# Retention values of all four heads projected in one unit of 512-column products, and gate units in another order, in a hybrid retention and block-attention layer

## Chip, cores and metric

The kernel runs on one core of a Trainium2 chip, as one program. The metric is the device time of one execution in microseconds (us).

## What is computed

The reference is one decoder layer for 512 tokens of width 1024, in float32. Cut to what matters:

```python
h = rmsnorm(x, norm1_w)
rq, rk, rv, rg, mq, mk, mv, ga, gb = split(h @ w_in)      # 512 512 1024 1024 512 512 512 1024 1024 columns
ret = silu(rg) * retention(rotary(rq), rotary(rk), rv)    # 4 heads, key width 128, value width 256
a = ret @ w_ret_out
b = moba_attention(rmsnorm(mq), rmsnorm(mk), mv) @ w_moba_out   # 8 heads of width 64
x = x + (sigmoid(ga) * a + sigmoid(gb) * b) @ w_o
h2 = rmsnorm(x, norm2_w)
x = x + (silu(h2 @ w_ffn_gate) * (h2 @ w_ffn_up)) @ w_ffn_down
```

The retention values `rv` are 1024 columns of `h @ w_in`, 256 for each head. The retention of a head takes scores of its rotated queries and keys (`rq`, `rk`), weights them by decay, and multiplies them with its values. The gates `ga` and `gb` are needed where `a` and `b` are mixed.

## The kernel before

**The units.** Everything outside attention and retention is a matrix product, and the kernel cuts it into units. Most units are one 2-by-2 block product done in seven block products instead of eight (Winograd's form of Strassen's method), named B11, B21, T1, T2, B22, T3 and T4. A block product takes its weights as one "piece" (or two) of 128 x 1024 numbers, which a DMA brings from HBM into a raw tile (`raw`); for T1 and T3 a second DMA on GpSimd's queue adds another quarter to it. To keep float32 accuracy, each piece is split into a rounded high part (`wh`, a cast on ScalarE, L418) and the rest (`wl`, a subtraction on VectorE, L222); the activations are held in the same two parts, and each product is three matmuls (`mm3`, L467): high by high, high by low, low by high. All matmuls, and all VectorE operations, are recorded at L222, a helper's line.

**Shapes.** For most units a matmul streams 256 columns. A unit of kind W (`rk`, `ga`, `gb`) holds the weights still and streams 256 tokens. A unit of kind X (`rv`, `rg`) holds tokens still and streams 256 columns of weights. A unit of 256 columns does 7 block products of 24 matmuls, 168 in all. A "wide" X unit (`mv` with the first half of `rg`, L1479, and the output projections) streams 512 columns and covers twice the columns with the same 168 matmuls; each of its block results takes two banks of PSUM instead of one, and its pieces are twice as many.

**The order of the work.** The code is written out in the order in which each engine runs it (the schedule is manual, and every engine takes its instructions in the order of the code). `ORDER` (L45) lists the units between attention's inputs and the output projection. Inside a unit, a string such as `NORMAL` (L80) gives the order of the seven products; what stands behind the slash (T4) is run inside the next unit, at its `*1`. Behind every half block product, that is 12 matmuls of 256 columns, comes one slot: `advance` (L435) takes a step of the clock called tick here, prepares at most one more piece, and `run_bg` (L718) takes one item from the list `bg`. The work of attention and of retention stands in that list, so that it is spread over the units; `later(n, f)` (L263) puts f off by n ticks. In the feed units `b` and `a` (`feat_blocks`, L753) a slot comes behind 12 matmuls of 512 columns.

**Attention** starts behind the `mv` unit, as 38 steps (`att_step`, L1159): products with masks, VectorE's row maximum (`mx`, `nb`), ScalarE's exponential (`p`, L1108), VectorE's scaling, TensorE's transposes into PSUM (`ps`), ScalarE's copies of them (`pt`, L1140 and L1145), and products with the values. PSUM has eight banks here, handed round; a unit that starts needs a bank that attention has given back.

**Retention before.** The unit `rv` 0 gives the values of heads 0 and 1, `rv` 1 those of heads 2 and 3. When the last quarter of such a unit is out (`rv_out`, L1258), the scores (`ret_scores`, L1285) and products (`ret_values`, L1315) of its two heads go into `bg`. By then the rotated queries and keys of those heads (`rk` 0 or `rk` 1, `rot_out`, L1216, tiles `rot`, `rH`, `rL`) have long been ready, for `rk` stands ahead of `rv`. When all is in, `ret_finish` (L1374) adds the normalisation (`ret_norm`) and the transposes (`ret_transpose`) into the tiles `ret`, which `a` multiplies.

**Gates.** `gate_unit` (L1395) multiplies each quarter by the token's norm on VectorE (`qa`, `qb` by `r1b`) and takes a tanh on ScalarE (L1405).

Of the kernel before, what the change touches and what calls it, by code (L numbers as in the profile page):

```python
# [13 lines left out]
ALU = mybir.AluOpType  # L14
# [25 lines left out]
STARTERS = 2  # L40
EXTRA = 1
WIDE = 4
OEXTRA = 5
FEXTRA = -2
ORDER = (("rk", 0), ("rv", 0), ("gb", 0), ("rk", 1), ("rv", 1), ("rg", 1), ("gb", 1), ("b", 0), ("b", 1), ("ga", 0), ("a", 0), ("ga", 1), ("a", 1))  # L45
RLAG = (1, 2, 3)
SLAG = (1, 1, 1)
ROT = 1
# [32 lines left out]
ENDING = "B11 T1 *1 T2 B21 B22 T3 T4w"  # L81
PLAIN = "B11 B21 B12 B22"
DOWN = "B11 B21 T1 T2 B22 T3 / T4"
ALONE = "B11 B21 T1 T2 B22 T3 T4z"


def weight_plan():

    units = []

    def feat(blocks):
        assert len(blocks) % 16 == 0  # L100
        for i in range(0, len(blocks), 16):
            units.append(("F", blocks[i:i + 16]))

    def group(name, col, kts):
        return [(name, k * P, col) for k in range(kts)]

    def wino(name1, col1, name2, col2, order=NORMAL):
        quarters = ((name1, col1, 0), (name2, col2, 0), (name2, col2, 4), (name1, col1, 4))
        units.append(("W", [(n, (k0 + k) * P, c + i * P) for n, c, k0 in quarters for i in (0, 1) for k in range(4)],
                      order))  # L110

    halves = (range(4), range(4, 8))

    def cols(col):
        units.append(("X", ("w_in", halves, (col, col + 256), 256), NORMAL))

    units += [("M", (C_MQ, 0)), ("M", (C_MQ, 4)), ("M", (C_MK, 0)), ("M", (C_MK, 4))]
    units.append(("X", ("w_in", halves, (C_MV, C_RG), 512), NORMAL))
    for name, i in ORDER:
        if name == "rg":  # L120
            cols(C_RG + 512 * i)
        elif name == "rv":
            cols(C_RV + 512 * i)
        elif name == "rk":
            wino("w_in", C_RQ + 256 * i, "w_in", C_RK + 256 * i)
        elif name == "a":
            feat(sum([group("w_ret_out", (4 * i + ct) * P, KT) for ct in range(4)], []))
        elif name == "b":
            feat(sum([group("w_moba_out", (4 * i + ct) * P, 4) for ct in range(4)], []))
        else:  # L130
            c = {"ga": C_GA, "gb": C_GB}[name] + 512 * i
            wino("w_in", c + 256, "w_in", c)
    units.append(("X", ("w_o", halves, (0, 512), 512), ALONE))
    for c in range(len(CHUNKS)):
        fs = chunk_tiles(c)
        for f in fs[::2]:
            order = ENDING if f == fs[-2] else NORMAL
            if f < 4:
                order = (PLAIN, DOWN)[f // 2]
            wino("w_ffn_gate", f * P, "w_ffn_up", f * P, order)  # L140
        units.append(("X", ("w_ffn_down", (fs[::2], fs[1::2]), (0, 512), 512), ALONE if c == len(CHUNKS) - 1 else DOWN))
    return units
# [27 lines left out]
def hybrid_block(ctx: ExitStack, tc: tile.TileContext, wall, xin, xtok, n2, cin, out):  # L170
# [652 lines left out]
    def wino_unit(w, ev, hooks={}):  # L823

        u = cur[0]
        cur[0] += 1
        order = plan[u][2].split()
        wide = plan[u][0] == "X" and plan[u][1][3] == 512
        banks = {}

        def bank(b):
            if b not in banks:
                z = zbank if b == "Z" else main_ps()
                banks[b] = [z, zbanks.pop() if b == "Z" and len(zbanks) > 1 else main_ps()] if wide else z
            return banks[b]

        def third(*x):
            ev.c22(*x)
            if "T4w" in order:
                ev.u3(*x)  # L840

        def first(*x):
            ev.p1(*([*x, bank("Z")] if seed else x))

        whole = "T4w" in order or "T4z" in order
        seed = order[1] != "B21"
        table = {"B11": ("X", "A11", True, False, first), "T1": ("Y", "S1", True, False, ev.p5),
                 "T2": ("X", "S2", False, False, ev.u2), "B21": ("Z", "A12", not seed, True, ev.c11),
                 "B22": ("Y", "S4", False, True, ev.c12), "T3": ("X", "S3", False, whole, third),
                 "T4": ("X", "A22", False, True, ev.c21),  # L850
                 "T4w": ("W", "A22", True, True, getattr(ev, "c21w", None)),
                 "T4z": ("Z", "A22", False, True, ev.c21)}

        def run(q):
            b, m, start, stop, out = table[q]
            wino_prod(w, u, bank(b), m, q.rstrip("wz"), start, stop, out,
                      (lambda i: ev.u3(bank("X"), i, bank("Z"))) if q == "T3" and "T4z" in order else None,
                      q == "T4z")

        rest = False  # L860
        for q in order:
            if q == "/":
                rest = True
            elif q[0] == "*":
                for _ in range(int(q[1:])):
                    wino_finish()
            elif rest:
                wpend.append(lambda q=q: run(q))
            else:
                run(q)  # L870
                if q in hooks:
                    hooks[q]()
# [53 lines left out]
    class WideQuarters:  # L926


        def __init__(self, out):
            self.out = out  # L930
            self.tiles = big(nm("qa")), big(nm("qb"))
            self.a, self.b = ((t[:, :512], t[:, 512:]) for t in self.tiles)

        def p1(self, x, i, z):
            A.copy(z[i], x[i])

        def p5(self, y, i):
            A.activation(self.a[i], y[i], AF.Copy, scale=-1.0)
# [2 lines left out]
            A.activation(self.b[i], x[i], AF.Copy, scale=-1.0)  # L941

        def c11(self, z, i):
            self.out(0, 0, i, z[i])

        def c12(self, y, i):
            V.tensor_tensor(self.b[i], self.b[i], y[i], ALU.subtract)
# [268 lines left out]
    def rot_out(h0):  # L1216
        def f(r, c, x):

            a, b = halves(nm("rot"))
            hf = RDK // 2  # L1220
            cos, sin = (y[:, r * 256:(r + 1) * 256].unsqueeze(1).to_broadcast([P, 2, 256]) for y in (cosT, sinT))
            part = {}

            def turn():
                A.copy(b[:hf], x[hf:])
                A.copy(b[hf:], x[:hf])

            def same():
                V.tensor_tensor(two(a), two(x), cos, ALU.mult)

            def high():
                if (c, h0) not in rT:
                    H, L = big(f"rH{c}_{h0}", F32R), big(f"rL{c}_{h0}", F32R)
                    rT[c, h0] = H, L
                    for i in (0, 1):
                        s = slice(i * 512, (i + 1) * 512)
                        (rqT, rkT)[c][h0 + i] = Two(H[:, s], L[:, s])
                part["H"], part["L"] = (two(y)[:, :, r * 256:(r + 1) * 256] for y in rT[c, h0])
                A.copy(part["H"], two(a))

            d = lane_start(LANE)
            if c == 0 or d == 0:
                turn()
            else:
                later(d, turn)
            later(1 if c == 0 else d + 1, same)
            later(d + 1, lambda: V.tensor_tensor(two(b), two(b), sin, ALU.mult))
            later(d + 2, lambda: V.tensor_tensor(a, a, b, ALU.add))
            later(d + 3, high)
            later(d + 4, lambda: V.tensor_tensor(part["L"], two(a), part["H"].bitcast(F32), ALU.subtract))  # L1250
        return f

    rqT, rkT = {}, {}
# [1 line left out]

    rv = {}

    def rv_out(h0):  # L1258
        def f(pair, i, x):
            rv[h0 + i, pair] = split(f"rv{h0 + i}_{pair}", x, None, 0 if i == 0 else SLAG[1])  # L1260
            if (pair, i) == (1, 0):
                a, b = ([lambda h=h, j=j: ret_scores(h, j) for j in range(NT)] for h in (h0, h0 + 1))
                v, w = ([lambda h=h, p=p: ret_values(h, p) for p in range(2)] for h in (h0, h0 + 1))
                fs = gates(h0 // 2)
                bg.extend(a + fs[:3] + v + b + [fs[3], None, None] + w + [None])
                ret_done("rv")
        return f


    sk = small("sk", RH * NT, 1)  # L1270
# [44 lines left out]
    def ret_values(h, pair):  # L1315
        ps = side_ps()
        for i in (2 * pair, 2 * pair + 1):
            c = (i % 2) * 256
            for j in range(i + 1):
                key, off = sc_off[j]  # L1320
                o = off + (i - j) * P
                mm3(ps[:, c:c + 256], tuple(x[:, o:o + P] for x in sc[h, key]),
                    rv[h, j // 2][:, (j % 2) * 256:(j % 2) * 256 + 256], j == 0, j == i)
        def stats():
            for i in (0, 1):
                bs = tp.tile([P, 6], F32, name=nm("bs"), tag="bs", bufs=4)
# [55 lines left out]

    def rk_unit(n):
        wino_unit(hW, Quarters(rot_out(2 * n)))

    def rv_unit(n):
        wino_unit(hW, Quarters(rv_out(2 * n)))


    sga, sgb, mixT = {}, {}, {}  # L1390
# [74 lines left out]
    def branch(cts, n, mov, evac):  # L1465
# [2 lines left out]
        feat_blocks(blocks[:n] + [wino_finish] + blocks[n:])  # L1468

    make = {  # L1470
        "rg": rg_unit, "rk": rk_unit, "rv": rv_unit,
        "ga": lambda n: gate_unit(sga, 4 * n),
        "gb": lambda n: gate_unit(sgb, 4 * n),
        "a": lambda n: branch(range(4 * n, 4 * n + 4), KT, retT, a_evac),
# [4 lines left out]
    wino_unit(hW, mv_ev)  # L1479
    more_raws(-WIDE)  # L1480
    for name, n in ORDER:
        make[name](n)
    assert not bg


# [362 lines left out]
```

## Time and profile before

| | |
|---|---|
| median of 3 runs | 778.76 us (778.73 to 779.47) |
| the profiled execution, its own time | 778.7 us |
| its span in the trace | 776.9 us, so 1.8 us lie around it |
| TensorE busy (PE) | 770.0 us of the span, 5224 matmuls |
| VectorE busy (DVE) | 630.8 us |
| ScalarE busy (ACT) | 454.9 us |
| granted TensorE clock | 1.00 |
| DMA | 134.85 MB, 174 GB/s on average |

PE is TensorE multiplying, PEld its loading of the stationary operand, DVE VectorE, ACT ScalarE, POOL GpSimd, SP the engine that issues most DMAs. A row of the timeline gives the start in us, the duration in us, the engine, the line, the operation, what it writes and reads, its form, and how many were merged; in brackets stands idle time ahead of it and who ended it. The durations of matmuls overlap, so the cost of one in a stream is read from start to start.

### The profile page before, as it was taken

What the parts mean: (1) busy time and instruction counts of PE and PEld (TensorE: products, weight loads), DVE (VectorE), ACT (ScalarE), POOL (GpSimd) and SP (SyncE); (2) the same over time, 40 slices, a digit from 0 to 9 for tenths busy, and PEclk for the clock granted to TensorE, in tenths of its full rate; (3) what the DMA queues carried; (4) which work ended last, traced back from release to release, by engine and by line L of the source; (5) the groups of instructions that cost most, each with busy time, mean ns of one, the idle gap of its engine ahead of it and who ended that gap; (6) DMA issues with size and microseconds to landing.
All of it is one profiled execution on the core that took longest, in us unless ns stands there. A gap on an engine that the chain in (4) does not pass through costs nothing.

```text
span 776.9 us, 13317 instructions
## 1 busy us (share of the span) xinstructions
PE 770.0 (99%) x5224; PEld 702.0 (90%) x5224; DVE 630.8 (81%) x959; ACT 454.9 (59%) x746; POOL 68.9 (9%) x83
## 2 busy tenths in 40 slices
PE   9999999999999999999999999999999999999997
PEld 6888888889999998989988899989999899988995
DVE  7988688887797677758589898899787977789786
ACT  8656587876675485734356675645554455655451
POOL 0001000000101000000001000111001110110000
PEclk9999999999999999999999999999999999999999
DMA  9947542536768474654899614779556993779502
GB/s 329 359 120 188 129 83 62 140 104 159 192 167 199 118 216 114 166 133 130 249 330 258 171 41 110 193 200 297 157 146 153 271 261 99 174 202 293 119 2 109
DMA packets 40959, 134.85 MB, mean 174 GB/s; under 512 B 4544, under 2 KB 5568, under 8 KB 40896
## 3 DMA queue, kind: packets, MB, share of 16 engines
q1 hardware_dynamic: 29088, 94.41, 34.3%
q0 software_dynamic: 11376, 39.06, 28.7%
q8 instruction: 41, 0.67, 0.3%
q10 hardware_dynamic: 432, 0.52, 0.2%
q14 instruction: 22, 0.18, 0.1%
HBM read 131.88 MB, written 2.10 MB: 172 GB/s over the span
## 4 chain that ended last, share of the span: by engine, by line
PE 91%; DVE 4%; ACT 3%; issue 1%; DMA 0%; SPq 0%; ACTq 0%; DVEq 0%
PE pm L222 84%; PE ps L222 8%; DVE h L222 1%; DVE ws L222 1%; DVE wl L222 1%; ACT wh L418 1%; DMA raw<-wall 0%; ACT f L1587 0%; DVE mx L222 0%; ACT p L1108 0%; DVE rot L222 0%; ACT h L1575 0%; DVE gsl L222 0%; ACT L1694 0%; ACT L1108 0%
## 5 line engine op out<-in xcount | busy, mean ns | idle before, releaser
L222 DVE TENSOR_TENSOR wl<-raw,wh 128x1024 fp32r<-128x1024 f32 x209 | 252.3, 1220 | 46.4 <-ACT wh L418 39.6
L418 ACT CAST wh<-raw 128x1024 fp32r<-128x1024 f32 (+1 forms) x230 | 225.5, 1008 | 58.3 <-DVE raw L222 32.3
L222 PE MATMUL pm<-h,wh 128*128 128x256 f32 x1248 | 225.3, 283 | 0.2 <-ACT fa L1660 0.2
L222 PEld LDWEIGHTS pm<-h,wh 128*128 128x128 f32 x1248 | 195.1, 192 | 0.9 <-ACT fa L1660 0.4
L222 PE MATMUL pm<-h,wl 128*128 128x256 f32 x624 | 176.6, 283 | 0.0
L222 PEld LDWEIGHTS pm<-h,wl 128*128 128x128 f32 x624 | 119.7, 192 | 0.0
L345 POOL DMA_DIRECT2D raw<-wall x60 | 53.3, 888 | 451.7 <-DMA raw<-wall 239.2
L222 PE MATMUL pm<-hS,wh 128*128 128x256 f32 x384 | 71.6, 286 | 0.0
L222 PE MATMUL pm<-wh,hA 128*128 128x256 f32 (+1 forms) x256 | 66.7, 337 | 0.0
L222 PEld LDWEIGHTS pm<-hS,wh 128*128 128x128 f32 x384 | 60.0, 191 | 0.3 <-issue 0.2
L222 PE MATMUL pm<-wh,hS 128*128 128x256 f32 (+1 forms) x256 | 57.2, 311 | 0.0
L222 PE MATMUL pm<-hS,wl 128*128 128x256 f32 x192 | 54.3, 283 | 0.0
L222 PE MATMUL pm<-hA,wh 128*128 128x256 f32 x288 | 53.6, 285 | 0.0
L222 DVE TENSOR_TENSOR raw<-raw,raw 128x1024 f32<-128x1024 f32 (+1 forms) x41 | 48.1, 1180 | 0.4
L222 PEld LDWEIGHTS pm<-wh,hA 128*128 128x128 f32 x256 | 44.4, 190 | 4.1
L222 PEld LDWEIGHTS pm<-hA,wh 128*128 128x128 f32 x288 | 45.2, 191 | 0.9 <-issue 0.3
L222 PEld LDWEIGHTS pm<-wh,hS 128*128 128x128 f32 x256 | 42.8, 190 | 2.8 <-issue 0.2
L222 PE MATMUL pm<-wl,hA 128*128 128x256 f32 (+1 forms) x128 | 42.2, 330 | 0.0
L222 PE MATMUL pm<-hA,wl 128*128 128x256 f32 x144 | 40.7, 283 | 0.0
L222 PE MATMUL pm<-wh,gsh 128*128 128x512 f32 x112 | 39.8, 390 | 0.0
L222 PE MATMUL pm<-wl,hS 128*128 128x256 f32 (+1 forms) x128 | 39.6, 309 | 0.0
L222 PE MATMUL pm<-ret,wh 128*128 128x512 f32 x128 | 39.5, 390 | 0.0
(257 smaller groups left out, 1380.1 us busy)
## 6 DMA issues: line engine op xcount, KB each, us to landing
raw<-wall SPq DMA_DIRECT2D x155, 512.0 KB, 5.1
raw<-wall POOLq DMA_DIRECT2D x70, 512.0 KB, 6.8
raw<-wall SPq DMA_DIRECT2D x21, 256.0 KB, 4.5
raw<-wall POOLq DMA_DIRECT2D x9, 256.0 KB, 7.6
xr<-xtok SPq DMA_DIRECT2D x4, 512.0 KB, 7.5
x<-xin SPq DMA_DIRECT2D x7, 256.0 KB, 5.5
out<-xr SPq DMA_DIRECT2D x7, 256.0 KB, 2.1
cs<-cin SPq DMA_DIRECT2D x1, 512.0 KB, 5.5
```

Source lines behind the costliest of these rows:

```text
L222: return f(out, *args, **kw)
L345: nc.gpsimd.dma_start(t[:, s], wall[c, :, s], accum_op=ALU.add)
L418: A.copy(h, src)
```

## The change

`ORDER` changes from

- `rk` 0, `rv` 0, `gb` 0, `rk` 1, `rv` 1, `rg` 1, `gb` 1, `b` 0, `b` 1, `ga` 0, `a` 0, `ga` 1, `a` 1

to

- `rk` 0, `gb` 0, `rvv`, `rg` 1, `rk` 1, `gb` 1, `b` 0, `b` 1, `ga` 0, `ga` 1, `a` 0, `a` 1.

`rvv` is a wide X unit for all 1024 value columns. Its product order `EARLIER` takes B11 and then B21 ahead of T1, with the T4 of the unit before it between them. In this order B11's result isn't copied into the bank in which B21 adds to it; it is kept in a tile `qc` and added to B21's result on VectorE. The second column half (heads 2 and 3) is split into its parts 40 ticks later (`VLAG`). Two more raw tiles are in flight during the unit (`WIDE2`). The work of heads 0 and 1 enters `bg` when the unit's last quarter is out, that of heads 2 and 3 when the last rotated quarter of `rk` 1 is ready.

```diff
+WIDE2 = 2
+VLAG = 40
+EARLIER = "B11 *1 B21 T1 T2 B22 T3 / T4"
...
+        elif name == "rvv":
+            units.append(("X", ("w_in", halves, (C_RV, C_RV + 512), 512), EARLIER))
...
-        def p1(self, x, i, z):
-            A.copy(z[i], x[i])
+        def p1(self, x, i, z=None):
+            if z:
+                A.copy(z[i], x[i])
+                return
+            if i == 0:
+                self.first[0], self.first[1] = halves(nm("qc"))
+            A.copy(self.first[i], x[i])
...
         def c11(self, z, i):
-            self.out(0, 0, i, z[i])
+            if not self.first:
+                self.out(0, 0, i, z[i])
+                return
+            f = self.first.pop(i)
+            V.tensor_tensor(f, f, z[i], ALU.add)
+            later(1, lambda: self.out(0, 0, i, f))
...
+            if (r, c, h0) == (1, 0, 2):
+                later(d + 5, lambda: ret_heads(2))
...
+    def rv_unit():
+        def out(r, c, i, x):
+            t = 2 * r + i
+            later(VLAG if c else 0, lambda: keep(c, t, x))
+            if (r, c, i) == (1, 0, 1):
                 ret_done("rv")
+                ret_heads(0)
+        def keep(c, t, x):
+            y = split(f"rv{c}_{t}", x, None, SLAG[1])
+            for h in (0, 1):
+                rv[2 * c + h, t] = y, h * 256
+        wino_unit(hW, WideQuarters(out))
+    def ret_heads(h0):
+        a, b = ([lambda h=h, j=j: ret_scores(h, j) for j in range(NT)] for h in (h0, h0 + 1))
+        v, w = ([lambda h=h, p=p: ret_values(h, p) for p in range(2)] for h in (h0, h0 + 1))
+        fs = gates(h0 // 2)
+        if h0:
+            bg.extend(a + fs[:3] + v + b + fs[:3] + w)
+            ret_done("rv")
+        else:
+            bg.extend(a + fs[:3] + v + b + [fs[3], None, None] + w + [None])
...
+        if name == "rvv":
+            more_raws(WIDE2)
         make[name](n)
+        if name == "rvv":
+            more_raws(-WIDE2)
```

Two places of the new order follow. The names in the rows are tiles with the number of their buffer; lines behind the change are 5 to 30 higher than before (L489 is L494 there, L1405 is L1435, L418 is L423).

The first place is ScalarE while TensorE ends the second unit of the list and is about to start the third one (before `gb` 0, now `rvv`). Before the change its queue reads:

```order
L1108 ACTIVATE p_1802,l<-ps_1778,nb,qs 128x128
L489 CAST rv_0_1820<-pm_236 128x512
L1108 ACTIVATE p_1834,l<-ps_1777,nb,qs 128x256
L1108 ACTIVATE p_1834,l<-ps_1778,nb,qs 128x256
L1239 CAST rH_0_1395<-rot_1660 128x2x256
L418 CAST wh_1854<-raw_1585 128x1024
L1140 COPY pt_1632<-ps_1856 128x2x128
L1145 COPY pt_1634<-ps_1856 128x256
```

With the change the same stretch reads:

```order
L1123 ACTIVATE p_1801,l<-ps_1777,nb,qs 128x128
L1123 ACTIVATE p_1832,l<-ps_1776,nb,qs 128x256
L1123 ACTIVATE p_1832,l<-ps_1777,nb,qs 128x256
L1254 CAST rH_0_1395<-rot_1659 128x2x256
L1435 ACTIVATE qa_1421<-qa_1421 128x512
L423 CAST wh_1852<-raw_1585 128x1024
L1155 COPY pt_1631<-ps_1854 128x2x128
L1160 COPY pt_1633<-ps_1854 128x256
```

The cast of values ahead of the two exponentials is gone, and a gate's tanh stands between the exponentials and the last copy. That copy reads `ps_1856` (now `ps_1854`), whose bank the first product of the third unit takes.

The second place is VectorE and TensorE where the feed unit `b` 0 starts. Before, VectorE's queue ahead of the first low weights of `b` 0 (`wl_3516`) reads:

```order
L222 TENSOR_TENSOR wl_3434<-raw_3012,wh_3417 128x1024
L222 BN_STATS bs_3462<-ps_3438 128x6
L222 BN_AGGR mvs<-bs_3462 128x2
L222 BN_STATS bs_3465<-ps_3438 128x6
L222 BN_AGGR mvs<-bs_3465 128x2
L222 TENSOR_TENSOR qa_3210<-pm_236,r1b 128x512
L222 BN_STATS bs_3509<-ps_3472 128x6
L222 BN_AGGR mvs<-bs_3509 128x2
L222 BN_STATS bs_3512<-ps_3472 128x6
L222 BN_AGGR mvs<-bs_3512 128x2
L222 TENSOR_TENSOR wl_3516<-raw_3185,wh_3470 128x1024
```

With the change the rows ahead of the first low weights of `b` 0 (`wl_3191`) read:

```order
L227 TENSOR_TENSOR wl_3118<-raw_2824,wh_3099 128x1024
L227 TENSOR_TENSOR rv_1_3102<-qb_1944,rv_1_3102 128x512
L227 TENSOR_TENSOR rot_3080<-rot_3080,cs 128x512
L227 TENSOR_TENSOR rot_3080<-rot_3080 128x512
L227 TENSOR_TENSOR qa_2956<-pm_236,r1b 128x512
L227 TENSOR_TENSOR wl_3152<-raw_2695,wh_3136 128x1024
L227 TENSOR_TENSOR rv_2_3156<-qa_1943,rv_2_3156 128x512
L227 TENSOR_TENSOR rL_2_2952<-rot_3080,rH_2_2951 128x2x256
L227 TENSOR_TENSOR qb_2957<-qb_2957,pm_2995 128x512
L227 TENSOR_TENSOR wl_3191<-raw_2937,wh_3172 128x1024
```

And TensorE's queue at that point, now:

```order
L227 MATMUL pm_2958<-hS_533,wl_3118 128x256
L227 MATMUL ps_3212<-rH_2_2951,rH_2_3022 128x512
L227 MATMUL ps_3212<-rL_2_2952,rH_2_3022 128x512
L227 MATMUL ps_3212<-rH_2_2951,rL_2_3023 128x512
L227 MATMUL pm_3218<-moT_1381,wh_3172 128x512 x2
L227 MATMUL pm_3218<-moT_1381,wl_3191 128x512
```

The last rotations of `rk` 1 (`rot`, `rL`) and the delayed splits of the values of heads 2 and 3 (`rv`) stand now directly ahead of `b` 0 on VectorE. The first score of head 2 (`ps_3212`), which reads the last of the rotated tiles (`rL_2_2952`), stands ahead of the first product of `b` 0. Before, the scores of head 2 came during `rg` 1 and `gb` 1.

More of the change, by code (lines that the diff above doesn't have):

```diff
@@ L42 @@
 WIDE = 4
+WIDE2 = 2
+VLAG = 40
 OEXTRA = 5
 FEXTRA = -2
-ORDER = (("rk", 0), ("rv", 0), ("gb", 0), ("rk", 1), ("rv", 1), ("rg", 1), ("gb", 1), ("b", 0), ("b", 1), ("ga", 0), ("a", 0), ("ga", 1), ("a", 1))
+ORDER = (("rk", 0), ("gb", 0), ("rvv", 0), ("rg", 1), ("rk", 1), ("gb", 1), ("b", 0), ("b", 1), ("ga", 0), ("ga", 1), ("a", 0), ("a", 1))
 RLAG = (1, 2, 3)
@@ L845, in wino_unit @@
         whole = "T4w" in order or "T4z" in order
-        seed = order[1] != "B21"
+        seed = [q for q in order if q[0] not in "*/"][1] != "B21"
         table = {"B11": ("X", "A11", True, False, first), "T1": ("Y", "S1", True, False, ev.p5),
@@ L929, in __init__ @@
         def __init__(self, out):
-            self.out = out
+            self.out, self.first = out, {}
             self.tiles = big(nm("qa")), big(nm("qb"))
             self.a, self.b = ((t[:, :512], t[:, 512:]) for t in self.tiles)
-        def p1(self, x, i, z):
-            A.copy(z[i], x[i])
+        def p1(self, x, i, z=None):
[5 more added lines that the diff above has]
+            A.copy(self.first[i], x[i])
         def p5(self, y, i):
@@ L1256, in hybrid_block @@
     rv = {}
[L1258 to L1265, printed above, removed]
-                ret_done("rv")
-        return f
+    def rv_unit():
[3 more added lines that the diff above has]
+            if (r, c, i) == (1, 0, 1):
+                ret_done("rv")
+                ret_heads(0)
[13 more added lines that the diff above has]
+            bg.extend(a + fs[:3] + v + b + [fs[3], None, None] + w + [None])
     sk = small("sk", RH * NT, 1)
@@ L1322, in ret_values @@
                 mm3(ps[:, c:c + 256], tuple(x[:, o:o + P] for x in sc[h, key]),
-                    rv[h, j // 2][:, (j % 2) * 256:(j % 2) * 256 + 256], j == 0, j == i)
+                    rv[h, j][0][:, rv[h, j][1]:rv[h, j][1] + 256], j == 0, j == i)
         def stats():
@@ L1384, in rk_unit @@
         wino_unit(hW, Quarters(rot_out(2 * n)))
-    def rv_unit(n):
-        wino_unit(hW, Quarters(rv_out(2 * n)))
     sga, sgb, mixT = {}, {}, {}
@@ L1470, in hybrid_block @@
     make = {
-        "rg": rg_unit, "rk": rk_unit, "rv": rv_unit,
+        "rg": rg_unit, "rk": rk_unit, "rvv": lambda n: rv_unit(),
         "ga": lambda n: gate_unit(sga, 4 * n),
```

## The prediction

> **What bounds the kernel now.** I read the page's busy shares first, then its chain, then TensorE's waits, then the windows around the units that change.
>
> ```profile
> PE 770.0 (99%) x5224; PEld 702.0 (90%) x5224; DVE 630.8 (81%) x959; ACT 454.9 (59%) x746; POOL 68.9 (9%) x83
> ...
> PE 91%; DVE 4%; ACT 3%; issue 1%; DMA 0%; SPq 0%; ACTq 0%; DVEq 0%
> ```
>
> TensorE is busy 99% of the span and 91% of the chain that ends last. The waits, TensorE's own (columns: total us, how often, the longest):
>
> ```profile
> PE ps L549 <- DVE warm L222: 1.2, 1, 1.2
> PE ps L222 <- ACT p L1108: 0.4, 1, 0.4
> PE ps L222 <- ACT pt L1145: 0.3, 1, 0.3
> ```
>
> Only 0.4 and 0.3 us in attention, and the 1.2 us of the start, are of any size. So there is almost no wait to remove. The change can gain only by making TensorE's own stream shorter, and lose only by making it wait. The windows over the units between `rk` 0 and `a` 0 (columns: window, its length, busy us with instructions of PE, PEld, DVE, ACT, POOL, then PE's granted clock, the DMA share and GB/s) show how near the helpers are to that:
>
> ```profile
> 126.00:146.00 20.00, 19.70 (x162) 16.58 (x161) 17.17 (x42) 17.70 (x42) 1.73 (x2) 1.00 0.54 129
> 140.00:180.00 40.00, 40.00 (x328) 34.42 (x325) 32.65 (x66) 29.98 (x71) 2.60 (x3) 1.00 0.55 138
> 220.00:260.00 40.00, 40.00 (x331) 39.87 (x330) 30.42 (x41) 24.99 (x39) 5.19 (x6) 1.00 0.73 186
> 280.00:300.00 20.00, 20.00 (x133) 18.43 (x132) 17.80 (x36) 19.21 (x31) 1.73 (x2) 1.00 0.79 211
> 300.00:340.00 40.00, 40.00 (x266) 36.61 (x265) 27.02 (x35) 20.64 (x31) 2.60 (x3) 1.00 0.53 148
> ```
>
> TensorE is full in all but the first. VectorE runs at 68% to 89% and ScalarE at 52% to 96%, so what matters is where several of their operations come together just ahead of something that TensorE needs. The clock is 1.00 throughout and no DMA is near its limit: DMA enters no term.
>
> **Term 1, the products.** Two stretches of the chain in order of time (start, us, what) give the price of a matmul in an unbroken stream, the first with 512 columns, the second with 256:
>
> ```profile
> 53.76 16.35 PE pm L222 x72
> ...
> 215.29 31.68 PE pm L222 x264
> ```
>
> 16.35 / 72 = 0.2271 us, and 31.68 / 264 = 0.1200 us. Two of 256 cost 0.2400, so a pair merged into one saves 0.0129 us. `rv` 0 and `rv` 1 hold 2 x 168 = 336 matmuls of 256 columns; the wide unit does the same in 168 of 512. 168 x 0.0129 = 2.17, so **-2.2 us**. TensorE's other work is the same in kind and number. From the two prices, a matmul has about 0.013 us beside its columns (0.2400 - 0.2271), and that is all that the merge takes away. [...]
>
> **Term 2, the start of `rvv`.** The third unit's first product takes the bank that the last probabilities' copies (`pt`) give back. ScalarE, VectorE and TensorE there before (timeline: start, us, engine, line, operation):
>
> ```profile
> 153.63 0.57 ACT L1108 ACTIVATE p<-ps,nb,qs 128x256 f32<-128x256 f32 x1 [1.35 <-DVE nb L222]
> ...
> 154.73 0.61 ACT L1239 CAST rH<-rot 128x512 fp32r<-128x512 f32 x1
> 155.24 1.05 ACT L418 CAST wh<-raw 128x1024 fp32r<-128x1024 f32 x1
> 156.19 0.38 ACT L1140 COPY pt<-ps 128x256 f32<-128x256 f32 x1
> 156.45 0.38 ACT L1145 COPY pt<-ps 128x256 f32<-128x256 f32 x1
> ```
>
> ```profile
> 151.52 1.22 DVE L222 TENSOR_TENSOR wl<-raw,wh 128x1024 fp32r<-128x1024 f32 x1
> 152.65 0.75 DVE L222 TENSOR_REDUCE mx<-ps 128x1 f32<-128x256 f32 x2
> 153.43 0.16 DVE L222 SCALAR_TENSOR_TENSOR nb<-mx,qs 128x2 f32<-128x2 f32 x1
> 153.51 0.68 DVE L222 TENSOR_TENSOR rv<-pm,rv 128x512 fp32r<-128x512 f32 x1
> 154.11 0.15 DVE L222 RECIPROCAL rl<-l 128x2 f32<-128x2 f32 x1
> ```
>
> ```profile
> 157.04 0.48 PE L222 MATMUL pm<-hA,wh 128*128 128x256 f32 x2
> ```
>
> The copy ends at 156.45 + 0.38 = 156.83, and the product starts at 157.04: 0.21 us of slack. ScalarE had waited 1.35 us for VectorE's `nb`, so the cast of `rv` ahead of that lay in idle time; taking it away brings nothing. Two things now come into the chain. On VectorE the gate's multiplication (`qa` by `r1b`) stands ahead of the low weights and the row maxima; by the 128x512 form above (153.51 to 154.11) it is 0.60 us, and the exponentials start that much later. On ScalarE the gate's tanh stands between the exponentials and the copies; by the cast of the same shape (154.73 to 155.24) it is 0.51. 0.60 + 0.51 - 0.21 = **+0.9 us** of a wait for the `pt` copy. Bounds: 0.3, if VectorE fits the multiplication into idle time and only the tanh counts, and 1.3, if the first 512-column products also go slower. Queued behind that product on TensorE is all of `rvv`, so nothing makes up for it. [...]
>
> **Term 3, the start of `b` 0.** The scores of head 2 stood inside `rg` 1; now the first stands between `gb` 1 and `b` 0, behind the last rotations. Before:
>
> ```profile
> 244.94 2.36 DVE L222 TENSOR_TENSOR wl<-raw,wh 128x1024 fp32r<-128x1024 f32 x2 [0.20 <-ACT wh L418]
> ...
> 283.63 1.20 DVE L222 TENSOR_TENSOR wl<-raw,wh 128x1024 fp32r<-128x1024 f32 x1
> ```
>
> ```profile
> 288.08 0.63 PE L222 MATMUL pm<-moT,wh 128*128 128x512 f32 x2
> 288.55 0.39 PE L222 MATMUL pm<-moT,wl 128*128 128x512 f32 x1
> ```
>
> The low weights were ready at 284.83, 3.7 us ahead of their product at 288.55. (Two of them back to back take 2.36, so they follow each other by 1.14 and last 1.22.) Now, from the end of the last quarter of `rk` 1 to that score, TensorE has four block products, 96 x 0.1200 = 11.5 us. VectorE has, up to the last low rotation (`rL_2_2952`), 9 operations of 512 columns (0.60 to 0.68) and 2 of 1024 (1.14 to 1.22): 7.7 to 8.6 us, so 2.9 to 3.8 us to spare; and up to `b` 0's low weights one more of each, 9.4 to 10.5 us, against 11.5 and five matmuls of 0.2271, 12.6: 2.1 to 3.2. That holds if VectorE starts in step, and this I can't read: ScalarE, which feeds it, is 96% busy in 280:300, and some of these operations wait for products of `gb` 1 in between. TensorE waited nothing in 280:300 and 0.3 us in 126:146, the two nearest rows. I take **+0.3 us**; the lower bound is 0, since no wait stood here that could go, and the upper 1.5, if the helpers are over four operations late (2.9 + 1.5 = 4.4 us).
>
> **Term 4, the start of `a` 0 and small edits.** `ga` 1 now lies between `ga` 0 and `a` 0. The last transposes of `ret` before:
>
> ```profile
> 325.99 0.60 PE L222 MATMUL ps<-cst,ro 128*128 128x128 f32 x4
> 326.63 0.59 ACT L489 CAST ret<-ps 128x512 fp32r<-128x512 f32 x1 [0.79 <-PE ps L222]
> 327.25 0.69 DVE L222 TENSOR_TENSOR ret<-ps,ret 128x512 fp32r<-128x512 f32 x1 [0.97 <-ACT ret L489]
> ...
> 333.62 0.63 PE L222 MATMUL pm<-ret,wh 128*128 128x512 f32 x2
> ```
>
> From the transposes to the low part takes 1.95 us, and `a` used it 5.7 us later. Now they end closer to `a`: its first nine products of 512 columns, 2.0 us, stand ahead of the first use of the last low part. That just holds when both engines are free, and not behind a 1.2 us subtraction. The two added subtotals (`qc`, two VectorE additions of 0.68) hide beside products: VectorE is at 82% in 140:180. The splits of the second half, 40 ticks later, are the same operations moved, and 220:260 has 24% of VectorE and 38% of ScalarE free for them. The pieces of `rvv` are as many as those of `rv` 0 and 1 (the same weights in 1024-number pieces), and their DMAs on SP's and GpSimd's queues only change places; at a share of 0.54 to 0.79 two more raw tiles suffice. Without that cover each late piece would cost about its 1.1 us cast. For all this **+0.2 us**, between 0 and 0.5.
>
> **Sum.** The profiled execution took 778.7 us, the median of the runs is 778.76, so no correction is needed. 778.7 - 2.2 + 0.9 + 0.3 + 0.2 = **777.9 us**.
>
> **Rivals.** A measurement of this kernel can tell about 0.2%, 1.6 us, from no change: faster is below 777.2, slower above 780.3.
>
> *No new wait.* `rvv` starts as smoothly as `rv` 1 did, VectorE finding room for the multiplication: 778.7 - 2.2 = 776.5. For it: the full windows above, and that TensorE's waits were tiny even in the two windows where the helpers are busiest. Against: the slack of 0.21 us is less than either operation that stands in the way. Half-way between, with one of the two starts free, it is near 777. Chance of below 777.2: 0.34.
>
> *A helper behind at `b` 0 (slower).* Hold-ups of the helpers in these windows before:
>
> ```profile
> 252.94 1.23 DVE L222 TENSOR_TENSOR wl<-raw,wh 128x1024 fp32r<-128x1024 f32 x1 [2.93 <-PE pm L222]
> 266.97 0.59 ACT L1331 COPY ro<-ps 128x512 f32<-128x512 f32 x1 [6.91 <-DVE bs L222]
> ```
>
> VectorE stood for 2.93 us behind a product, ScalarE 6.91 behind VectorE, and neither cost TensorE anything, for the weights were made ahead. At `b` 0 the first score reads VectorE's newest result. If a hold-up like ScalarE's falls there, what exceeds the smaller spare time, 6.91 - 2.9 = 4.0 us, is TensorE's in place of 0.3: 777.9 - 0.3 + 4.0 = 781.6. It costs something once the helpers are 2.9 us behind, and makes the kernel slower once all waits together pass 1.6 + 2.2 = 3.8 us, with 1.1 of terms 2 and 4 at 2.9 + 2.7 = 5.6 us behind. Against: VectorE idles 11% to 32% in these windows and can catch up. Chance 0.15.
>
> *The merge saves less.* The 0.013 us may hang on what surrounds a matmul in those two stretches rather than on the matmul. [...] Against it: in both stretches TensorE runs the same mix of three matmuls, without a gap, at the same clock. Chance 0.04. [...]
>
> That the change does not do what it says is excluded: TensorE's queue holds 168 matmuls of 512 columns more and 336 of 256 fewer.
>
> **How the numbers follow.** The forecast (waits of 0.7 to 3.8 us against 2.2) has 0.47, the merge that saves less 0.04: together 0.51 for no change. Faster has 0.34, slower 0.15. With terms 2 to 4 at their low ends (0.3, 0, 0) the time is 776.8, and without any wait 776.5; with all at their high ends (1.3, 1.5, 0.5) it is 779.8. To leave out no more than 2 in 10 the range goes from 776.3, just below the case without a wait, to 780.4, a little over the high ends and into the foot of the slower case.
>
> **What would show it.** In the new profile: 168 fewer matmuls on TensorE; 512-column streams at 0.227 us each in `rvv`; a wait of TensorE for a `pt` copy of 0.5 to 1.3 us near 157 us; one for `rL` or `rH`, or for `b` 0's weights, of up to 1.5 us where `b` 0 starts; one of up to 0.5 us for `ret` at `a` 0; no other. No wait at `rvv` would make term 2 wrong; a wait over 2 us at `b` 0 would make term 3 wrong; waits for `raw` would mean that the DMAs, which I cost at nothing, decide. A time below 776 would mean a gain that I don't see at all.

## The result and the profile after

The changed kernel takes 787.09 us (median of 5 runs, 786.17 to 788.72) against 778.87 before (median of 5): 1.0103 times the time, 95% interval 1.0092 to 1.0114. It is 8.2 us slower; forecast were 777.9 us and a range up to 780.4. The profiled execution took 786.47 us, its span is 784.5 (before 776.9), so the traces below differ by 7.6 us.

The first line of the profile's page shows that the merge was made: 5224 - 168 = 5056 matmuls.

```profile
PE 771.4 (98%) x5056; PEld 694.1 (88%) x5056; DVE 631.5 (80%) x961; ACT 455.5 (58%) x746; POOL 68.7 (9%) x83
```

The products cost what was forecast. An unbroken stretch of the wide unit in the timeline (start, us, engine, line, operation), first and last row; between them lie 25 groups of three:

```profile
185.21 0.62 PE L227 MATMUL pm<-wh,hS 128*128 128x512 f32 x2
...
202.21 0.39 PE L227 MATMUL pm<-wh,hS 128*128 128x512 f32 x1
```

17.00 / 75 = 0.2267 us each. At these prices the sum of all matmuls is 2.2 us less than before. The rest of the change in time is waits and a lower clock. TensorE's own waits, which were 0.4 us and less apart from the 1.2 us of the start:

```profile
PE pm L227 <- ACT pm L907: 2.6, 1, 2.6
PE ps L227 <- DVE rL L227: 1.8, 1, 1.8
PE ps L554 <- DVE warm L227: 1.2, 1, 1.2
PE pm L227 <- DVE wl L227: 1.2, 2, 0.6
PE pm L227 <- DVE mh L227: 1.1, 1, 1.1
PE ps L227 <- ACT p L1123: 0.4, 1, 0.4
PE pm L227 <- ACT pt L1160: 0.3, 1, 0.3
```

The 1.1 us for `mh` stand 6 us after the start, where both kernels run the same work; the traces of the experiments have it at anything from nothing to 0.9. Where the others stand, in TensorE's timeline (in brackets the idle time and who ended it):

```profile
158.46 0.50 PE L227 MATMUL pm<-wh,hA 128*128 128x512 f32 x1 [0.35 <-ACT pt L1160]
279.45 0.50 PE L227 MATMUL ps<-rL,rH 128*128 128x512 f32 x1 [1.75 <-DVE rL L227]
281.18 0.80 PE L227 MATMUL pm<-moT,wl 128*128 128x512 f32 x1 [0.54 <-DVE wl L227]
298.51 0.50 PE L227 MATMUL pm<-moT,wl 128*128 128x512 f32 x1 [0.64 <-DVE wl L227]
323.15 0.50 PE L227 MATMUL pm<-hS,wh 128*128 128x256 f32 x2 [2.59 <-ACT pm L907]
```

These are the start of `rvv`, the first score of head 2 ahead of `b` 0, `b` 0's first low weights, the start of `b` 1, and the third product of `ga` 0. From start to start, less the price of a matmul in a stream, they cost 0.5, 1.9, 0.7, 0.8 and 2.75 us, 6.7 in all.

At the stops of `b` 0 the granted clock fell (windows: length, busy us of PE, PEld, DVE, ACT, POOL, then the clock):

```profile
280.00:282.00 2.00, 1.46 (x5) 0.91 (x4) 2.00 (x3) 0.84 (x1) 0.00 (x0) 0.68 0.69 258
282.00:284.00 2.00, 2.00 (x6) 1.52 (x6) 1.19 (x3) 2.00 (x6) 0.38 (x1) 0.50 0.02 8
284.00:286.00 2.00, 2.00 (x13) 1.83 (x12) 1.22 (x2) 2.00 (x7) 0.48 (x1) 0.96 0.38 47
```

At 0.50 a 512-column matmul takes 0.427 us from start to start instead of 0.227; summed over the matmuls from 281 to 284.3 us that is 1.5 us more. So 6.7 + 1.5 - 2.2 = 6.0 of the 7.6 us are named. The other 1.6 are small pieces: 0.5 lies ahead of 100 us, where both kernels run the same work; some 0.8 are delays of TensorE at 262 and 274 us, each too short for a row of its own among the waits; and the rest I did not follow.

Why VectorE was late at `b` 0 is seen when the windows of the two kernels are laid beside each other. Before:

```profile
190.00:225.00 35.00, 35.00 (x290) 34.87 (x289) 26.42 (x50) 22.11 (x38) 4.33 (x5) 1.00 0.57 140
255.00:281.00 26.00, 26.00 (x215) 25.87 (x214) 17.34 (x36) 14.88 (x29) 1.73 (x2) 1.00 0.54 143
```

After:

```profile
190.00:225.00 35.00, 35.00 (x219) 31.77 (x218) 18.86 (x21) 16.19 (x22) 3.45 (x4) 1.00 0.69 174
255.00:281.00 26.00, 23.84 (x186) 22.42 (x184) 24.49 (x32) 19.04 (x28) 1.73 (x2) 0.99 0.54 148
```

Between 190 and 225 us (now the second half of the wide unit and the start of `rg` 1) VectorE lost 7.6 us of work; in the 26 us ahead of `b` 0 it gained 7.2 and is busy 94%. The same windows for the tile `rot` alone name the work (busy of VectorE, then of ScalarE). Before:

```profile
190.00:225.00 35.00, 5.32 (x8) 4.08 (x7) 1.00 0.57 140
225.00:255.00 30.00, 5.33 (x8) 3.21 (x6) 1.00 0.82 208
255.00:281.00 26.00, 0.00 (x0) 0.00 (x0) 1.00 0.54 143
```

After:

```profile
225.00:255.00 30.00, 0.00 (x0) 0.12 (x1) 1.00 0.65 160
255.00:281.00 26.00, 10.65 (x16) 7.16 (x12) 0.99 0.54 148
```

All four rotations of `rk` 1, 16 operations of VectorE, now stand in those 26 us; before, they were spread over 65. Three of the four delayed splits of the values (`rv`) stand there too, the fourth ends at 281.7 us. VectorE's timeline there, from the last rotation to `b` 0's low weights:

```profile
271.32 0.68 DVE L227 TENSOR_TENSOR rot<-pm,cs 128x512 f32<-128x512 f32 x1
...
278.71 0.69 DVE L227 TENSOR_TENSOR rL<-rot,rH 128x512 fp32r<-128x512 f32 x1
...
279.91 1.22 DVE L227 TENSOR_TENSOR wl<-raw,wh 128x1024 fp32r<-128x1024 f32 x1
```

TensorE had the last quarter of `rk` 1 ready at 265.4, 11.9 us ahead of the score at 277.30. VectorE took it up at 271.32, 5.9 us later, and needed 8.1 us from there to `rL` (279.40).

The stop in `ga` 0 is another one. ScalarE's queue ahead of it:

```profile
319.26 0.47 ACT L1337 ACTIVATE sc<-ps,sk 128x256 fp32r<-128x256 f32 x1 [1.74 <-DVE dia L227]
319.63 0.29 ACT L1340 CAST sc<-dia 128x128 fp32r<-128x128 f32 x1
321.11 0.37 ACT L1337 ACTIVATE sc<-ps,sk 128x128 fp32r<-128x128 f32 x1 [1.18 <-DVE dia L227]
321.37 1.03 ACT L423 CAST wh<-raw 128x1024 fp32r<-128x1024 f32 x1
...
322.51 0.59 ACT L907 COPY pm<-pm 128x512 f32<-128x512 f32 x1
```

The copy of the unit's first block result (L907), which the third product waits for, stands behind the score operations (`sc`) of head 3, and these wait twice for VectorE. In this trace the copy does not pass them: it waits out 2.9 us (1.74 + 1.18) in which ScalarE idles for operations ahead of it.

The 0.8 us at `b` 1 are a third case. VectorE was not full there; it had stood idle for a product of TensorE just before it made the low weights in question:

```profile
297.23 1.23 DVE L227 TENSOR_TENSOR wl<-raw,wh 128x1024 fp32r<-128x1024 f32 x1 [2.59 <-PE pm L227]
```

### The profile page after: what moved, and what is told of

Same layout as the page of the kernel before. It is cut to its first block, busy times and chain, and to the rows that moved or that the text cites. A ratio compares the mean times of both kernels' runs of the same rounds, so it can differ in the third digit from the quotient of the medians.

```text
span 784.5 us, 13007 instructions
## 1 busy us (share of the span) xinstructions
PE 771.4 (98%) x5056; PEld 694.1 (88%) x5056; DVE 631.5 (80%) x961; ACT 455.5 (58%) x746; POOL 68.7 (9%) x83
## 4 chain that ended last, share of the span: by engine, by line
PE 58%; DVE 4%; ACT 2%; issue 1%; DVEq 0%; ACTq 0%
PE pm L227 56%; PE ps L227 2%; DVE wl L227 1%; DVE h L227 1%; DVE ws L227 1%; ACT f L1621 0%; ACT wh L423 0%; ACT h L1609 0%; DVE gsl L227 0%; ACT L1728 0%; DVE qa L227 0%; DVE raw L227 0%; DVE fb L227 0%; DVE gs L227 0%; DVE rv L227 0%
## 5 line engine op out<-in xcount | busy, mean ns | idle before, releaser
L423 ACT CAST wh<-raw 128x1024 fp32r<-128x1024 f32 (+1 forms) x230 | 225.7, 1009 | 76.5 <-DVE raw L227 30.3
L227 PE MATMUL pm<-wh,hA 128*128 128x512 f32 (+1 forms) x208 | 64.7, 375 | 0.3 <-ACT pt L1160 0.3
L227 PE MATMUL pm<-wh,hS 128*128 128x512 f32 (+1 forms) x192 | 52.1, 354 | 0.0
L227 PEld LDWEIGHTS pm<-wh,hA 128*128 128x128 f32 x208 | 37.9, 189 | 6.8 <-ACT pt L1160 0.6
L227 PEld LDWEIGHTS pm<-wh,hS 128*128 128x128 f32 x192 | 34.3, 189 | 5.1
L227 PE MATMUL pm<-wl,hA 128*128 128x512 f32 (+1 forms) x104 | 38.1, 366 | 0.0
L227 PEld LDWEIGHTS pm<-hS,wl 128*128 128x128 f32 x192 | 36.7, 191 | 0.2 <-DVE wl L227 0.2
```

What stands on the lines that cost most here:

```text
L227: return f(out, *args, **kw)
L423: A.copy(h, src)
```

## The experiments

The theory after the result (A): VectorE is over-full ahead of `b` 0, since the rotations and the delayed splits come together there. Rivals: the order of the gates (B), the wide unit (C), the place of the first score (D), ScalarE. Times are medians, each with its ratio to the kernel before, run beside it; stops are given as above, from start to start. (The expectations name 3.0 us for the stops at `b` 0 and 1.3 for the dip of the clock; read from start to start they are 2.6 and 1.5.)

**The gate order alone**, on the kernel before:

```diff
-ORDER = rk 0, rv 0, gb 0, rk 1, rv 1, rg 1, gb 1, b 0, b 1, ga 0, a 0, ga 1, a 1
+ORDER = rk 0, gb 0, rv 0, rk 1, rv 1, rg 1, gb 1, b 0, b 1, ga 0, ga 1, a 0, a 1
```

> The kernel before with the gate units reordered alone (gb 0 ahead of rv 0, ga 1 ahead of a 0); the values stay in two units of 256 columns, rk 1 stays ahead of rv 1 and rg 1. Theory A (what costs is that the last rotations of rk 1 and the delayed splits come directly ahead of b 0, so that VectorE is late there): nothing of that moves, 778.5 to 779.8 us, waits of TensorE in the middle under 1 us in all. Rival B (the order of the gates itself costs, by the tanhs in attention and the later a 0): over 781, with waits at the third unit and at ga 0 or a 0. Rival C (the wide unit's pieces and banks cost): as A here.

780.92 us against 778.76, ratio 1.0027 (1.0017 to 1.0037): slower by 2.2, between the two expectations. Its stops are three:

```profile
PE ps L222 <- DVE sc L222: 0.4, 1, 0.4
PE pm L222 <- DVE qb L222: 0.4, 1, 0.4
...
PE pm L222 <- ACT pt L1145: 0.4, 1, 0.4
```

The last is the start of the third unit, 0.5 us, as in the changed kernel: it belongs to the gate in attention, not to the wide unit. The other two (0.6 each, at 229 and 245 us) are scores and quarters of `rv` that meet at another moment than before. So theory A is not all of it: the order of the gates costs by itself. Of this only the first 0.5 us is found again in the changed kernel, and no stop stands at `ga` 0 or `a` 0 here.

**The wide unit in the old order**, splits 12 ticks later:

```diff
-VLAG = 40
+VLAG = 12
+ORDER = rk 0, rvv, gb 0, rk 1, rg 1, gb 1, b 0, b 1, ga 0, a 0, ga 1, a 1
```

> The changed kernel with the wide unit in the place of rv 0, and all others in the order of before (rk 0, rvv, gb 0, rk 1, rg 1, gb 1, b, ga 0, a 0, ga 1, a 1); the second half is split 12 ticks later instead of 40, so that it is ready for the earlier scores. Theory A: the rotations of rk 1 are done a unit before b 0 again, 776.5 to 777.8 us, no wait at b 0 over 0.5 us, clock 1.00 throughout. Rival B (the gates): as A. Rival C (the wide unit): 780 or more, with TensorE waiting for wide pieces or banks in or behind rvv.

796.61 us, ratio 1.0227 (1.0214 to 1.0241). Theory A's expectation was wrong by 19 us; the time is where rival C had it (780 or more). In this place the wide unit lies inside attention, and there TensorE stops six times, 5.1 us in all: for `pt` three times, for `qc`, `p` and `moT` once each. Nor does the old place of `rk` 1 help: the code puts the first score of head 2 directly behind the last rotation, wherever that is, and TensorE waited there for ScalarE's and VectorE's newest results (3.95 us for `rH` and 1.1 for `rL`, at 267 us). A further 2.9 us stand in `b` 0, for `qb`.

```profile
PE ps L227 <- ACT rH L1254: 3.8, 1, 3.8
PE pm L227 <- DVE qb L227: 2.7, 1, 2.7
```

The run moves several things at once and so does not decide between the theories; it shows that the wide unit costs dearly inside attention. Against rival C speaks the changed kernel's own trace: there TensorE has no idle row at all from the start of `rvv` (158.46 us) to 276 us.

**Splits 16 ticks later instead of 40:**

```diff
-VLAG = 40
+VLAG = 16
```

> The changed kernel with the second half of the values split 16 ticks later instead of 40: four casts on ScalarE and four subtractions on VectorE (4 x 0.60 = 2.4 us) leave the stretch ahead of b 0. Theory A: the wait at the start of b 0 falls from 3.0 us to under 1 and the dip of the clock behind it (1.3 us) shrinks or goes; the wait of 2.75 us in ga 0 stays: 783 to 785 us. If VectorE's load is not the cause (the score's place or ScalarE is): 786 to 787.

789.88 us (ratio 1.0142, 1.0128 to 1.0156), slower than the changed kernel, against both expectations. The stops at `b` 0 did fall, from 2.6 to 1.4 us. But the splits now met the scores and values of heads 0 and 1: seven new stops between 231 and 279 us, 3.9 in all (one for `ro` of 1.2), and `ga` 0 grew to 3.3 us with a dip of the clock (0.59 in 322 to 328 us).

```profile
PE pm L227 <- ACT pm L907: 3.8, 2, 3.2
...
PE ps L227 <- ACT ro L1364: 1.1, 1, 1.1
```

**The first score two slots later:**

```diff
-                later(d + 5, lambda: ret_heads(2))
+                later(d + 7, lambda: ret_heads(2))
...
-            bg.extend(a + fs[:3] + v + b + fs[:3] + w)
+            bg.extend(a + fs[:1] + v + b + fs[:3] + w)
```

> The changed kernel with the first score of head 2 two slots later, so that it stands inside b 0 instead of ahead of it; two empty slots behind the scores are left out, so that all behind them keeps its place. Theory A (VectorE's throughput): the wait for rL goes, but b 0's low weights are no earlier, so TensorE waits 2.5 to 3 us for wl instead: 786 to 787.5 us. Rival D (the place of the score alone costs, since it asks for VectorE's newest result): the wait for rL goes and little takes its place, 783 to 784.5.

793.45 us, ratio 1.0189 (1.0172 to 1.0207). At `b` 0 rival D falls: the wait for `rL` went, and the same time came back as 1.4 us for the first product and 1.9 for its low weights (3.3, before 2.6). The total is worse than either expectation, by new stops of 1.4 and 1.0 us at 306 and 317 us, by the stop in `ga` 0, which grew to 3.5, and by a longer dip (0.50 in 280 to 286 us) and a second one (0.93 in 322 to 328).

```profile
PE pm L227 <- ACT pm L907: 3.3, 1, 3.3
PE pm L227 <- DVE wl L227: 1.7, 1, 1.7
PE pm L227 <- ACT wh L423: 1.2, 1, 1.2
PE ps L227 <- DVE sc L227: 1.2, 1, 1.2
```

**Less rotation** (8 of the 16 VectorE operations on `rot` of `rk` 1 left out, all else in the same order):

```diff
+            if h0:
+                later(d + 1, lambda: dve_cost(512))
+                later(d + 2, lambda: dve_cost(512))
+                later(1 if c == 0 else d + 1, lambda: V.tensor_tensor(two(a), two(x), two(b), ALU.add))
```

(`dve_cost` only keeps the planner's count, so that the pieces stay where they were.)

> The changed kernel without two of the three VectorE operations of each of the four rotations of rk 1 (cosine and sine multiplications; x and its turned half are added only): the rotation of heads 2 and 3 is left out in part, 8 x 0.60 = 4.8 us less on VectorE, most of it in the 26 us ahead of b 0, everything else in the same order. Theory A (VectorE is over-full ahead of b 0, 94% in 255 to 281 us): the 3.0 us of waits at the start of b 0, the dip of the clock behind them (1.3) and the 0.8 at b 1 go, the 2.75 in ga 0 stays: 781 to 783 us. If it is the place of the score, ScalarE or the DMAs: 785 or more.

783.54 us, ratio 1.0062 (1.0049 to 1.0074), 3.5 less than the changed kernel and a little above the expected 781 to 783. The 255 to 281 us of this run:

```profile
255.00:281.00 26.00, 25.91 (x201) 24.90 (x200) 21.08 (x29) 20.72 (x33) 1.73 (x2) 1.00 0.54 143
```

VectorE is busy 21.08 us instead of 24.49, TensorE 25.91 of 26; of 2.6 us at `b` 0 0.26 are left, and the clock stays at 1.00 there. The 0.8 at `b` 1 stayed, against the expectation, and the 2.75 in `ga` 0 stayed as expected, now with a dip behind it (0.72 in 319 to 325 us).

**Its counterpart, less work on ScalarE** (the two turning copies of each rotation of `rk` 1 left out):

```diff
-            if c == 0 or d == 0:
-                turn()
-            else:
-                later(d, turn)
+            if not h0:
+                if c == 0 or d == 0:
+                    turn()
+                else:
+                    later(d, turn)
```

> The changed kernel without the two ScalarE copies of each of the four rotations of rk 1 (the half turn is left out, the sine multiplication reads the unturned numbers), 8 x about 0.6 us = 4.8 us less on ScalarE, most of it ahead of b 0, all else in the same order: the counterpart of the run with less rotation, which took 4.8 us from VectorE there. Theory A (VectorE is the full one): the waits at the start of b 0 stay above 2 us and that in ga 0 at 2.7: 785 to 787.5 us. If ScalarE is as much the bound, or the two in turn: the waits at b 0 fall below 1 us as with less rotation: 782 to 784.5 us.

787.15 us (ratio 1.0104, 1.0084 to 1.0125; its six runs lie between 784.8 and 790.7, so the stops say more than the time). ScalarE had 4.1 us less to do in the same stretch, and the stops at `b` 0 (1.9 and 0.7), `b` 1 (0.8) and `ga` 0 (2.75) are what they were; a new one of 1.4 stands at 263 us, for `qb`, and one of 0.9 at 443:

```profile
255.00:281.00 26.00, 23.09 (x186) 22.48 (x185) 23.63 (x32) 14.91 (x21) 1.73 (x2) 1.00 0.53 140
```

Together the two runs settle the stop at `b` 0: it is VectorE's load, not ScalarE's. (Both leave out work that the result needs, so they are tests and no remedies.)

**Less rotation, and head 3's scores directly behind head 2's:**

```diff
-            bg.extend(a + fs[:3] + v + b + fs[:3] + w)
+            bg.extend(a + b + v + fs[:1] + w)
```

> As the run with less rotation, and the four scores of head 3 directly behind those of head 2, in b 0 instead of at the start of ga 0. Theory A with its second part (in ga 0 the copy of the first block result stands on ScalarE behind two score operations that wait for VectorE): the 2.75 us in ga 0 go too: 778 to 780.5 us. If the wait in ga 0 has another cause: as the run with less rotation.

781.66 us, ratio 1.0040 (1.0027 to 1.0053). The time misses the expected 778 to 780.5. The stop in `ga` 0 fell from 2.75 to 0.56 us, as the second part of the theory has it; a new one of 1.4 us opened at 299 us, where `b` 1 waits for a bank that the scores hold:

```profile
PE pm L227 <- DVE sc L227: 1.2, 1, 1.2
...
PE pm L227 <- ACT pm L907: 0.4, 1, 0.4
```

**Nothing left out: splits 48 ticks later**, without and with that move of the scores:

```diff
-VLAG = 40
+VLAG = 48
```

> The changed kernel with the second half of the values split 48 ticks later, so that most of these splits come behind the first products of b 0, where VectorE is 56% busy (281 to 313 us). Theory A: 2.4 us leave VectorE ahead of b 0, the waits there fall from 3.0 to about 0.6 us and the dip goes; the wait in ga 0 stays: 782.5 to 784.5 us. If only the sum of the work counts and every move opens a new wait, as 16 ticks did: 786 to 790.

> The changed kernel with both moves and nothing left out: splits 48 ticks later, and the scores of head 3 directly behind those of head 2. Theory A with its second part: 779.5 to 782 us, no wait of over 0.7 us left between 260 and 330 us. If every move opens a new wait: 784 or more.

785.78 us (1.0091, 1.0077 to 1.0104) and 785.73 (1.0087, 1.0073 to 1.0100). The first lies between its two expectations: the stops at `b` 0 are 1.4 us and the dip there is gone (1.00 in 278 to 286 us), but the values of head 2 now wait 1.9 us for a split, and a dip stands at `ga` 0 (0.72 in 322 to 328). In the second the 2.8 in `ga` 0 is 0.55, and 2.8 us of new stops stand in `b` 0 and `b` 1 and 0.9 at 263. The line of the first:

```profile
PE ps L227 <- DVE rv L227: 1.7, 1, 1.7
```

What theory A expected of the second is refuted: the move of the scores opened new waits that cost as much as it saved.

**Other orders of the units.** Here, and in the last run, the second half's scores start when both `rk` 1 and `rvv` are done (in these lists `rk` 1 is always the later one, so that this alone moves nothing):

```diff
+ORDER = rk 0, gb 0, rvv, gb 1, rk 1, rg 1, b 0, b 1, ga 0, ga 1, a 0, a 1
+VLAG = 24
```

> The changed kernel with gb 1 ahead of rk 1 and rg 1 behind it (rk 0, gb 0, rvv, gb 1, rk 1, rg 1, b 0 ...), and the second half of the values split 24 ticks later. The rotations of rk 1 and the scores of head 2 come a unit earlier; gb 1's products with the norm (4 x 0.60 us on VectorE) leave the 26 us ahead of b 0. Theory A (VectorE over-full ahead of b 0): no wait over 0.7 us at the start of b 0, and fewer in ga 0, since the scores of head 3 come before it: 778 to 782 us. If the sum of the moved work alone counts, the waits move to the scores in rg 1 and gb 1: 784 or more.

> The same order of units, with the second half split 40 ticks later as in the changed kernel, that is, at the first products of head 2. Theory A: the splits come when VectorE also has the scores of head 2, so 0.5 to 2 us slower than with 24 ticks: 779 to 784 us. If the sum alone counts: as with 24 ticks.

785.65 us (1.0087, 1.0073 to 1.0100) with 24 ticks, 787.03 (1.0108, 1.0094 to 1.0122) with 40. The expectation contained a slip: `rk` 1 is the last but one unit ahead of `b` 0 in this list too, so rotations and scores did not come earlier. What did move, four gate multiplications and (with 24 ticks) the splits, lowered the stops at `b` 0 to 0.7 us; with 40 ticks they are 1.9. The stop in `ga` 0 grew to 4.3 us in both: ScalarE's queue there has the same rows and the same two waits as above, but TensorE needed the copy 4.7 us earlier than in the changed kernel, and the copy came only 3.1 earlier (24 ticks; with 40 ticks 2.4 and 0.8). The clock fell to half there (24 ticks):

```profile
319.00:325.00 6.00, 4.96 (x23) 4.96 (x24) 2.87 (x5) 3.70 (x7) 0.00 (x0) 0.50 0.90 216
```

**No gate in attention:**

```diff
+ORDER = rk 0, rg 1, rvv, gb 0, rk 1, gb 1, b 0, b 1, ga 0, ga 1, a 0, a 1
```

> The changed kernel with rg 1 in attention and gb 0 behind the wide unit (rk 0, rg 1, rvv, gb 0, rk 1, gb 1, b 0 ...): no gate's multiplication or tanh stands ahead of the third unit any more. Term 2 of the prediction: the wait of 0.5 us at the start of the wide unit goes or falls to 0.2. Theory A: 4 x 0.60 us of gate products come on VectorE between the wide unit and b 0, so it is no earlier there: waits of 3 us or more at b 0 and 2.5 in ga 0 stay, 786 to 789 us. If the gates in attention are what costs: 780 or less.

784.47 us (1.0076, 1.0064 to 1.0089), below what theory A expected, and the fastest run with the wide unit that leaves nothing out. The stop at the start of `rvv` is gone, as term 2 says. `b` 0 stops 2.1 us instead of 2.6, for three operations of the rotations now come ahead of 255 us; `b` 1 (0.8) and `ga` 0 (2.75) are unchanged.

No version beat the kernel before, the gate order alone (780.92) included.

## Why the prediction was wrong

**Term 1 (-2.2) was right.** 0.2267 us a matmul against 0.2271 taken. That also ends the third rival.

**Term 2 (+0.9, 0.3 to 1.3) was right in mechanism.** The stop for the `pt` copy measured 0.5 us; it appears with the gate order alone and goes without a gate in attention.

**Term 3 (+0.3, 0 to 1.5) is the step that failed.** It counted VectorE's operations from the end of the last quarter of `rk` 1 on: 7.7 to 8.6 us to `rL`, and 8.1 were measured. The failing words are "That holds if VectorE starts in step". It started 5.9 us late. The prediction's own spare time of 2.9 to 3.8 us makes of that a wait of 2.1 to 3.0 us at the score, and 1.9 were measured there (2.6 with the low weights right behind it): the count was sound, but the lateness was put at next to nothing. VectorE was late because the 16 us ahead were nearly full too, 14.6 us busy against 10.5 in the same window before (first row before, second row now):

```profile
255.00:271.00 16.00, 16.00 (x132) 15.87 (x131) 10.50 (x22) 7.27 (x13) 1.73 (x2) 1.00 0.43 104
255.00:271.00 16.00, 15.97 (x133) 15.79 (x132) 14.62 (x19) 11.70 (x18) 1.73 (x2) 1.00 0.58 134
```

I judged them by windows of the kernel before (68% to 89% busy, "can catch up"), and those windows held other work: the change took `rk` 1 out of 190 to 255 us and put it into 255 to 281. The order told which 16 rotations and which splits come between the scores and `b` 0; adding their 0.6 us each to the window of before (17.3 + 16 x 0.6 + 4 x 0.6 = 29 of 26 us) would have warned of it, though it overstates: other work left the stretch, and 24.5 us were measured. Against +0.3 stand 2.6 us of stops and, in the profiled execution, 1.5 of the clock's dip. The 0.8 at `b` 1 stayed when VectorE was relieved, so it is not of this step.

**The slower rival had the right place with too small a chance.** It set the point from which `b` 0 waits at 2.9 us behind and the point from which the kernel is slower at 5.6; VectorE was 5.9 behind. It had 0.15. Its reason was another, a single hold-up of a helper and not an engine with too much to do, and it had nothing of `ga` 0; that its 4.0 us come near 2.6 + 1.5 at `b` 0 is luck.

**Term 4 (+0.2, up to 0.5) failed too, in the place.** At `a` 0 there is no stop for `ret`. The 2.75 us came in `ga` 0, where head 3's scores now stand ahead of the first copy on ScalarE. I costed the scores of heads 2 and 3 only where the first of them stands, not along the list `bg`; moving them (runs with both heads' scores together) takes the stop away. The copy had no cushion that I had looked at. The term also put the second half's splits where 220:260 has room; in the trace VectorE runs all four between 271.9 and 281.7 us, just ahead of `b` 0 and at its start, and putting them off by 8 ticks more took the stops there from 2.6 to 1.4 us.

**The clock** was taken as 1.00 throughout. At `b` 0 the stops of 2.6 us were followed by 1.5 us more of slow matmuls.

What stays open: the 1.6 us in small pieces; what holds `b` 1's low weights; and whether some order exists in which the wide unit keeps its 2.2 us. Later splits eased `b` 0 and the move of the scores eased `ga` 0, but each shifted the helpers' work onto another product.

## What to carry to other kernels

When a change moves units, take the helpers' work with them: sum the operations that the order puts into each stretch of some 25 us, and compare with the stretch, not with the busy share that the trace of before shows at that time. A stall-free matrix engine says nothing about how far the other engines are from stalling it; what tells it is how far ahead of its use each weight is ready, here 3.7 us before and nothing after. And every queue that a moved step joins has to be looked through for the copy behind it that the matrix engine needs next; here ScalarE's held head 3's scores ahead of the copy for which `ga` 0 stopped 2.75 us.

## What the runs showed of the hardware

In the changed kernel's trace the granted clock fell to 0.50 at `b` 0, behind the stop of 1.9 us and about when that of 0.7 began, for 3.4 us (by the three windows above, 1.28 + 2.00 + 0.16). The same two stops, 1.9 and 0.7 us, brought no dip in the run with less work on ScalarE:

```profile
279.00:286.00 7.00, 5.20 (x26) 4.26 (x27) 6.15 (x11) 5.08 (x11) 0.86 (x1) 1.00 0.25 89
```

At the single stop of 2.75 us in `ga` 0 the clock fell in the runs with less rotation and with no gate in attention (0.72 in 319 to 325 us of both), with 48 ticks (0.72 in 322 to 328) and with less work on ScalarE (0.95 in 313 to 345), and not in the changed kernel (1.00 in 319 to 328), though the stop is the same; at 4.3 us it fell in both runs (0.50 with 24 ticks and 0.61 with 40, in 319 to 325). So the length of a stop did not by itself tell whether the clock fell; what else decides it, these runs do not show.

The dips do not explain why the runs of the changed kernel spread over 2.5 us (786.17 to 788.72) and those of before over 0.7. The run whose mean clock was 1.000 took 787.14 us and one with 0.997 took 786.17, so an execution without a dip need not be a faster one; the 1.5 us above are read from the profiled execution alone.

Small moves were dear: of twelve edits around a schedule almost without stops, none came below the kernel before, and the best of those with the wide unit and all the work won back 2.6 of the 8.2 us.
